# Head output projections behind the next head's value groups, and the retention norm's steps further apart

## The chip, the cores and the metric

The kernel runs on one core of a Trainium2 chip. Its time is the device time of one execution in microseconds (us). Several executions are timed, and the median is quoted; one more execution is recorded by the hardware profiler, and all rows of the trace below come from that one.

## The reference, cut to what matters

Two layers work on 528 tokens (16 learned ones, then 512). Each projects the normed tokens with one large matrix, and has two branches on the slices of that projection: a gated short convolution and a retention with four heads.

```python
proj = rmsnorm(h, pre_norm_g[l]) @ w_in[l] + b_in[l]
c_h, c_b, c_c, c_z, r_q, r_k, r_v, r_z, g_a, g_b = split(proj)
# convolution branch
u = c_c * c_h
y_a = (c_b * (conv_b + taps(u)) * silu(c_z)) @ w_conv_out
# retention branch, for each of 4 heads (256 query/key columns, 512 value columns)
s = (rope(q) @ rope(k).T / 16) * decay       # scores, causal by chunks of 64
out = s @ v                                  # with the carried state
out = (out - mean(out)) * rsqrt(var(out) + 1e-5) * gn_g * silu(z)   # the norm, per token
y_b = concat(out of all heads) @ w_ret_out   # the output projection
# merge
h = h + rmsnorm((sigmoid(g_a) * y_a + sigmoid(g_b) * y_b) @ w_o[l], post_norm_g[l])
```

The mean over the values is taken out of v ahead of the product with the scores, so that the norm only has to find a sum of squares per token and multiply by its inverse root.

## The kernel before

**Precision.** Every product is made in three passes: each operand is split into a rounded high part and the rest (`whi` and `wlo` for weights, a pair `r` for activations). ScalarE casts the high part (L142) and VectorE subtracts it (L143). The three passes are high by high, high by low, and low by high.

**The large projection.** A `Group` makes 256 columns of it (K, Q, the two halves V0 and V1, and the two halves Z0 and Z1 of the gate, for each head; H, C, Z and B for each of four convolution groups). It uses a block scheme with seven products instead of eight. A product is one call of `mul` (L279): 12 matmuls, into the accumulators `pa`, `pb` or `pc`. ScalarE evicts them (`put`, L325, and the copy of bias into `pa`, L335). A Group needs four pairs of split weights, and sums of raw weight blocks that VectorE makes (L307, L314, L315).

**The output projection of a head** is four `RetOut` jobs, RO0 to RO3, of 48 matmuls each in layer 1 (in `mm_tile`, L244, two banks `pp`). It multiplies the normed and split output of the head (`yr`, four pairs `r`) with one pair of split weights.

**The order of the jobs** in a layer is one list, `todo`. For head 1 it reads K, Q, V0, then RO0 and RO1 of head 0, V1, RO2 and RO3 of head 0, Z0, Z1, and likewise for heads 2 and 3. This text calls these ten jobs the group of head 1, 2 or 3. Behind them comes convolution group 1, with the projection of head 3 between its last jobs, then convolution groups 2 and 3. The weights are loaded and split in the order in which the jobs are made: the four Groups of a convolution group first, then the RetOut jobs that stand between them. Six tiles hold raw weights and four pairs hold split ones, so a later load or split waits for a tile to come free.

**Steps of the retention** (rope, scores, product with the values, norm) do not stand in that list. They are queued with `later(n, step)`, and each `mul`, or each two steps of a RetOut product, is a tick; the step is issued n ticks after it was queued. When the last gate half Z1 is done, `z_done` queues the product with the values (`attend`) at ticks 1, 3, 5 and 7, and the norm behind it:

- `stats` at tick 10: a matmul with ones sums the squares over the partitions (L370), VectorE makes the mean (`nv`, L374), GpSimd raises it to the power -1/2 (`ny`, L375);
- `wide` at tick 13: a transpose on TensorE spreads `ny` (L384), ScalarE copies it out (L387);
- `finish(v)` at ticks 14 to 17: VectorE multiplies (L514), and the result is split into a pair `r` (L142, L143), which RO0 to RO3 then read.

A step falls so into the group of the next head: `stats` of head 0 in the group of head 1. The rope of K and Q (L403, L404, L405, then the split into `r`) is queued when K and Q are done; the scores (L422 on TensorE, L433 on VectorE) eight or more ticks behind Q.

**The last word on the order** is a static scheduler's. It takes the program in the order of issue and lays down one list for each engine by its own estimate; evictions by L325, some casts and the end of `attend` have a higher priority there. Each engine then works off its list strictly in that order.

Of the kernel before, what the change touches and what calls it, by code (L numbers as in the profile page):

```python
# [56 lines left out]
def trunk(ctx: ExitStack, tc: tile.TileContext, xT, w_in, binT, w_co, w_ro, w_o, gpre, gpost,  # L57
# [486 lines left out]
    def conv_group(l, i2, res):  # L544
        cs = slice(QCOLS[l].t0, T)
        cc = slice(14 if l else 0, T)
        st = {}

        def c_h(ts):
            st["h"] = ts  # L550

        def c_c(ts):
            st["u"] = []
            for s in range(2):
                u = gr.tile([P, T + 2], F32, tag="u", name=nm("u"), bufs=2)
                if l < DEPTH - 1:
                    nc.vector.memset(u[:, 0:2], 0.0)
                nc.vector.tensor_tensor(u[:, 2 + cc.start:], ts[s][:, cc], st["h"][s][:, cc], op=ALU.mult)
                i = i2 * 2 + s
                a = ts[s]  # L560
                w = lambda j: cw_sb[:, l, j, i:i + 1]
                nc.scalar.activation(a[:, cs], u[:, 2 + cs.start:2 + T], AF.Identity, scale=w(2), bias=cb_sb[:, l, i:i + 1])
                for j in (1, 0):
                    nc.vector.scalar_tensor_tensor(a[:, cs], u[:, j + cs.start:j + T], w(j), a[:, cs], op0=ALU.mult, op1=ALU.add)
                st["u"].append(a)

        def c_z(ts):
            nc.scalar.activation(ts[1][:, cs], ts[1][:, cs], AF.Silu)
            for a, t in zip(st["u"], ts):
                nc.vector.tensor_tensor(a[:, cs], t[:, cs], a[:, cs], op=ALU.mult)  # L570

        def c_b(ts):
            for a, t in zip(st["u"], ts):
                nc.vector.tensor_tensor(t[:, cs], t[:, cs], a[:, cs], op=ALU.mult)
                hi, lo = rslot(), rslot()
                split(hi[:, cs], lo[:, cs], t[:, cs])
                res.append((hi, lo))

        return [Group(l, C_H + i2 * 256, I_CONV[l], c_h), Group(l, C_C + i2 * 256, I_CONV[l], c_c),
                Group(l, C_Z + i2 * 256, I_Q[l], c_z, AF.Silu), Group(l, C_B + i2 * 256, I_Q[l], c_b)]  # L580

    class ConvOut:

# [212 lines left out]
    for l in range(DEPTH):  # L796
# [58 lines left out]
        def z_done(ts, hd, h, l, yr, silu=(1,)):  # L855
# [10 lines left out]
            later(0, start)  # L866
            for v in range(4):
                later(1 + 2 * v, lambda v=v: attend(l, h, *hd["S"], hd["V"], v, hd["zt"][v], hd["sums"]))
            later(10, lambda: hd["n"][0]())
            later(13, lambda: hd["n"][1]())  # L870
            for v in range(4):
                later(14 + v, lambda v=v: hd["n"][2](v))

        hd["done"] = (k_done, q_done, v_done, z_done)
        yrs = jb["yrs"] = [[] for _ in range(H)]
# [7 lines left out]
        for h in range(1, H):  # L883
            d = {}
            add(Group(l, R_K + h * DK, I_ALL[l], lambda ts, d=d: k_done(ts, d)))
            add(Group(l, R_Q + h * DK, I_Q[l], lambda ts, d=d, h=h, l=l: q_done(ts, d, h, l)))
            add(Group(l, R_V + h * DV, I_ALL[l], lambda ts, d=d: v_done(ts, d)))
            for q in (0, 1):
                add(RetOut(l, h - 1, q), yrs[h - 1])
            add(Group(l, R_V + h * DV + 256, I_ALL[l], lambda ts, d=d: v_done(ts, d)))  # L890
            for q in (2, 3):
                add(RetOut(l, h - 1, q), yrs[h - 1])
            for b in range(2):
                add(Group(l, R_Z + h * DV + b * 256, I_Q[l],
                          lambda ts, d=d, h=h, l=l, yr=yrs[h]: z_done(ts, d, h, l, yr), AF.Silu))
        for n, g in enumerate(conv_group(l, 1, conv)):
            add(g)
            if n >= 2:
                for q in (2 * n - 4, 2 * n - 3):
                    add(RetOut(l, H - 1, q), yrs[H - 1])  # L900
        add_conv(2)
        add_conv(3)

        def gate_b(ts, b, l=l):
            cs = slice(QCOLS[l].t0, T)
# [354 lines left out]
```

## Time and profile before

| | us |
|---|---|
| median of three timed executions | 1605.07 |
| lowest and highest of them | 1603.92, 1609.26 |
| the profiled execution | 1600.25 |
| its span in the trace | 1598.4 |

The span runs from the first to the last recorded instruction. In the profiled execution TensorE is busy for 1553.9 us, VectorE for 1168.9 us, ScalarE for 910.2 us and GpSimd for 28.9 us. A busy time is an average over stages that differ; the rows further down are read from single stages. In them a row of the timeline gives a start, a duration, the engine, the line, the operation with the tiles that it writes and reads, and in brackets how long the engine stood idle before it and what ended that.

### The profile page before, as it was taken

How to read it: one execution, taken by the hardware profiler on the slowest of the kernel's cores; microseconds unless marked ns; L12 is line 12 of the kernel's file. 1: busy time of each engine (PE TensorE's matmuls, PEld its weight loads, DVE VectorE, ACT ScalarE, POOL GpSimd, SP SyncE). 2: the span in 40 equal slices, each digit the busy share in tenths (PEclk: the TensorE clock that was granted, in tenths of full speed). 3: DMA queues.
4: the chain of work that ended last, by engine and by line, in shares of the span. 5: the costliest groups of instructions: out<-in, count | busy, mean ns of one | idle time of the engine just before them, and what ended most of it. 6: DMA issues, size and time to landing. Idle time of an engine off the chain costs nothing.

```text
span 1598.4 us, 29227 instructions
## 1 busy us (share of the span) xinstructions
PE 1553.9 (97%) x11762; PEld 1494.1 (93%) x11762; DVE 1168.9 (73%) x1702; ACT 910.2 (57%) x1763; POOL 28.9 (2%) x23
## 2 busy tenths in 40 slices
PE   9999999899999999999999999999999999999998
PEld 9989999898999999999999998998998999999986
DVE  6996966776776788866376889678777777997542
ACT  6675565464565466655345666655654655676531
POOL 0000000001000000000000000000000000000000
PEclk9999999999999999999999999999999999999999
DMA  7132332232222243335321223222322223334421
GB/s 263 67 113 73 106 107 89 83 108 97 89 103 87 91 141 128 133 123 180 119 101 53 100 94 113 103 103 95 111 93 80 101 98 119 132 126 145 142 98 53
DMA packets 86039, 174.37 MB, mean 109 GB/s; under 512 B 11280, under 2 KB 15888, under 8 KB 85904
## 3 DMA queue, kind: packets, MB, share of 16 engines
q1 hardware_dynamic: 85760, 172.50, 31.2%
q8 instruction: 92, 1.51, 0.4%
q14 instruction: 43, 0.35, 0.1%
q10 hardware_dynamic: 144, 0.01, 0.0%
HBM read 168.21 MB, written 4.26 MB: 108 GB/s over the span
## 4 chain that ended last, share of the span: by engine, by line
PE 79%; DVE 10%; ACT 5%; issue 3%; DMA 3%; POOL 1%; SPq 0%; DVEq 0%; POOLq 0%; ACTq 0%
PE pb L279 25%; PE pp L244 15%; PE pc L279 13%; PE pp L648 7%; PE pa L279 6%; PE pp L481 4%; PE pp L1122 3%; PE pb L648 3%; DVE wlo L143 2%; PE pp L422 2%; DMA raw<-in_w_in 2%; ACT whi L142 2%; DVE r L143 1%; PE pp L384 1%; PE pp L447 1%
## 5 line engine op out<-in xcount | busy, mean ns | idle before, releaser
L143 DVE TENSOR_TENSOR wlo<-raw,whi 128x1024 fp32r<-128x1024 f32 (+2 forms) x358 | 392.7, 1107 | 120.4 <-ACT whi L142 117.5
L142 ACT CAST whi<-raw 128x1024 fp32r<-128x1024 f32 (+2 forms) x358 | 339.4, 959 | 227.8 <-PE pp L244 63.7
L279 PE MATMUL pb<-Xh,whi 128*128 128x264 f32 (+2 forms) x1008 | 287.7, 285 | 2.2 <-ACT pa L335 1.2
L279 PE MATMUL pb<-Xl,whi 128*128 128x264 f32 (+2 forms) x1008 | 285.0, 283 | 0.0
L279 PE MATMUL pb<-Xh,wlo 128*128 128x264 f32 (+2 forms) x1008 | 284.7, 283 | 0.1
L244 PE MATMUL pp<-r,whi 128*128 128x264 f32 (+1 forms) x1152 | 251.2, 325 | 5.6 <-ACT r L142 4.8
L279 PE MATMUL pc<-Xh,whi 128*128 128x264 f32 (+2 forms) x672 | 194.4, 289 | 8.1 <-ACT f L325 7.8
L244 PEld LDWEIGHTS pp<-r,whi 128*128 128x128 f32 x1152 | 176.3, 188 | 23.7 <-ACT r L142 5.9
L279 PEld LDWEIGHTS pb<-Xh,whi 128*128 128x128 f32 x1008 | 189.6, 188 | 4.4 <-ACT pa L335 1.6
L279 PE MATMUL pc<-Xl,whi 128*128 128x264 f32 (+2 forms) x672 | 192.0, 286 | 0.0
L279 PE MATMUL pc<-Xh,wlo 128*128 128x264 f32 (+2 forms) x672 | 191.5, 285 | 0.0
L279 PEld LDWEIGHTS pb<-Xl,whi 128*128 128x128 f32 x1008 | 189.6, 188 | 0.6
L279 PEld LDWEIGHTS pb<-Xh,wlo 128*128 128x128 f32 x1008 | 189.3, 188 | 0.5 <-DVE wlo L143 0.3
L244 PE MATMUL pp<-r,wlo 128*128 128x264 f32 (+1 forms) x576 | 153.1, 321 | 1.4 <-DVE wlo L143 1.4
L307 DVE TENSOR_TENSOR raw<-raw 128x512 f32<-128x512 f32 x168 | 115.1, 686 | 41.4 <-DMA raw<-in_w_in 40.9
L279 PEld LDWEIGHTS pc<-Xh,whi 128*128 128x128 f32 x672 | 128.0, 190 | 12.3 <-ACT f L325 11.2
L279 PEld LDWEIGHTS pc<-Xl,whi 128*128 128x128 f32 x672 | 127.9, 190 | 0.4
L279 PEld LDWEIGHTS pc<-Xh,wlo 128*128 128x128 f32 x672 | 127.8, 190 | 0.3
L244 PEld LDWEIGHTS pp<-r,wlo 128*128 128x128 f32 x576 | 95.3, 188 | 9.8 <-DVE wlo L143 2.0
L279 PE MATMUL pb<-Xh,whd 128*128 128x264 f32 (+2 forms) x336 | 96.7, 288 | 1.1 <-ACT f L325 1.1
L279 PE MATMUL pa<-Xh,whi 128*128 128x264 f32 (+2 forms) x336 | 96.7, 288 | 0.0
L279 PE MATMUL pa<-Xl,whi 128*128 128x264 f32 (+2 forms) x336 | 95.7, 285 | 0.0
(219 smaller groups left out, 3300.3 us busy)
## 6 DMA issues: line engine op xcount, KB each, us to landing
raw<-in_w_in SPq DMA_DIRECT2D x426, 256.0 KB, 2.9
raw<-in_w_ro SPq DMA_DIRECT2D x32, 512.0 KB, 3.2
raw<-in_w_in SPq DMA_DIRECT2D x20, 512.0 KB, 4.8
raw<-in_w_co SPq DMA_DIRECT2D x16, 512.0 KB, 3.2
raw<-in_w_o SPq DMA_DIRECT2D x16, 512.0 KB, 3.9
Dsb<-in_decay SPq DMA_DIRECT2D x8, 520.0 KB, 3.9
h1d<-f SPq DMA_DIRECT2D x8, 264.0 KB, 4.5
f<-h1d SPq DMA_DIRECT2D x8, 264.0 KB, 4.3
```

The costliest lines, as they stand in the source:

```text
L142: nc.scalar.copy(dst_hi, src)
L143: nc.vector.tensor_tensor(dst_lo, src, dst_hi.bitcast(F32), op=ALU.subtract)
L244: nc.tensor.matmul(banks[i][:, 0:cols.n], wt(k)[:, msl], xs(k)[:, sl], start=(k == 0 and a == 0), stop=(k == nk - 1 and a == 2),)
L279: nc.tensor.matmul(o[:, 0:n], wt[:, k, :], xs[:, blk, k, HALF - n:], start=(first and k == 0 and a == 0), stop=(k == 3 and a == 2), skip_g ...
L307: nc.vector.tensor_tensor(r[:, 512:], r[:, 512:], r[:, 0:512], op=ALU.add)
L384: nc.tensor.matmul(pp[:, c // per, (c % per) * sc:(c % per + 1) * sc], y[:, c:c + 1].to_broadcast([sc, P]), ident[0:sc, 0:sc], start=True, ...
L422: nc.tensor.matmul(pp[0:kn, n + i, 0:cols.n], k[dt][x][:, k0:k0 + kn] if j < 4 else k8[:, dt * 2 + x, :], q[dt][y][:, sl], start=(dt == 0 ...
L447: nc.tensor.transpose(pp[0:kn, b, v * P:(v + 1) * P], vt[v][:, k0:k0 + kn] if j < 4 else v8[:, v, :], ident)
L481: nc.tensor.matmul(pp[:, b, lo_ - banks[b][0]:hi_ - banks[b][0]], V[j][x][0:kn, v * P:(v + 1) * P], S[0:kn, SOFF[j] + lo_ - q0:SOFF[j] + h ...
L648: nc.tensor.matmul(o, wt(k), xs[:, i0:], start=(k == 0 and a == 0), stop=(k == KD - 1 and a == 2))
L1122: nc.tensor.matmul(o, x[:, xs], wo[k][half][w], start=(k == 0 and a == 0), stop=(k == KD - 1 and a == 2))
```

## The change

Three things are edited. In a head's group, V1 moves ahead of RO0 and RO1, and Z0 stands between RO1 and RO2: the order is now K, Q, V0, V1, RO0, RO1, Z0, RO2, RO3, Z1. In the norm, `stats` goes from tick 10 to 11, `wide` from 13 to 17, and `finish(v)` from 14+v to 18+v. In the convolution part, groups 1 to 3 are one run of twelve Groups, and RO0 to RO3 of head 3 stand one by one behind the fourth to the seventh of them; `conv_group` has become a generator, so that the weights of each Group are queued when its turn comes.

```diff
-        return [Group(l, C_H + i2 * 256, I_CONV[l], c_h), Group(l, C_C + i2 * 256, I_CONV[l], c_c),
-                Group(l, C_Z + i2 * 256, I_Q[l], c_z, AF.Silu), Group(l, C_B + i2 * 256, I_Q[l], c_b)]
+        for col, i0, cb, act in ((C_H, I_CONV, c_h, AF.Identity), (C_C, I_CONV, c_c, AF.Identity),
+                                 (C_Z, I_Q, c_z, AF.Silu), (C_B, I_Q, c_b, AF.Identity)):
+            yield Group(l, col + i2 * 256, i0[l], cb, act)
...
-            later(10, lambda: hd["n"][0]())
-            later(13, lambda: hd["n"][1]())
+            later(11, lambda: hd["n"][0]())
+            later(17, lambda: hd["n"][1]())
             for v in range(4):
-                later(14 + v, lambda v=v: hd["n"][2](v))
+                later(18 + v, lambda v=v: hd["n"][2](v))
...
-            add(Group(l, R_V + h * DV, I_ALL[l], lambda ts, d=d: v_done(ts, d)))
-            for q in (0, 1):
-                add(RetOut(l, h - 1, q), yrs[h - 1])
-            add(Group(l, R_V + h * DV + 256, I_ALL[l], lambda ts, d=d: v_done(ts, d)))
-            for q in (2, 3):
-                add(RetOut(l, h - 1, q), yrs[h - 1])
             for b in range(2):
+                add(Group(l, R_V + h * DV + b * 256, I_ALL[l], lambda ts, d=d: v_done(ts, d)))
+            for b in range(2):
+                for q in (2 * b, 2 * b + 1):
+                    add(RetOut(l, h - 1, q), yrs[h - 1])
                 add(Group(l, R_Z + h * DV + b * 256, I_Q[l],
                           lambda ts, d=d, h=h, l=l, yr=yrs[h]: z_done(ts, d, h, l, yr), AF.Silu))
-        for n, g in enumerate(conv_group(l, 1, conv)):
+        for n, g in enumerate(g for i2 in (1, 2, 3) for g in conv_group(l, i2, conv)):
             add(g)
-            if n >= 2:
-                for q in (2 * n - 4, 2 * n - 3):
-                    add(RetOut(l, H - 1, q), yrs[H - 1])
-        add_conv(2)
-        add_conv(3)
+            if n in (3, 4, 5, 6):
+                add(RetOut(l, H - 1, n - 3), yrs[H - 1])
```

**TensorE, layer 2, group of head 1, between the first and the second product of V0.** `pb` and `pc` are the accumulators of V0, `pp` the two banks of RO0, and `r` the split output of head 0. Before (of 16 rows of L244, the first three and the last two stand here):

```order
L279 MATMUL pb_11706<-Xl,whi_11549 128x264
L279 MATMUL pb_11706<-Xh,wlo_11550 128x264
L244 MATMUL pp_11862<-r_11415,whi_11696 128x512
L244 MATMUL pp_11862<-r_11416,whi_11696 128x512
L244 MATMUL pp_11876<-r_11415,whi_11696 128x512
...
L244 MATMUL pp_11876<-r_11415,wlo_11697 128x512
L244 MATMUL pp_11876<-r_11433,whi_11696 128x512
L279 MATMUL pc_11707<-Xh,whi_11549 128x264
L279 MATMUL pc_11707<-Xl,whi_11549 128x264
```

After, at the same place:

```order
L279 MATMUL pb_11707<-Xl,whi_11545 128x264
L279 MATMUL pb_11707<-Xh,wlo_11546 128x264
L279 MATMUL pc_11708<-Xh,whi_11545 128x264
L279 MATMUL pc_11708<-Xl,whi_11545 128x264
L279 MATMUL pc_11708<-Xh,wlo_11546 128x264
```

The 16 matmuls of RO0 are gone from between the two products, and nothing has taken their place. In layer 1 it is the same with 30 matmuls of L244 (264 columns each). On VectorE, one more sum of weight blocks (L307) stands ahead of the last step of K's rope (L405) there, in both layers.

**TensorE, layer 1, group of head 2, around the sum of squares (L370).** `pc_3263` and `pb_3262` are the last two products of Q before, `pb_3263` the last product of Q after, and `pb_3476` the first product of V0 after. Before:

```order
L279 MATMUL pc_3263<-Xl,whi_3188 128x264
L279 MATMUL pc_3263<-Xh,wlo_3189 128x264
L370 MATMUL pp_3435<-ones_d,f_3148 88x1 x6
L279 MATMUL pb_3262<-Xh,whi_3188 128x264
L279 MATMUL pb_3262<-Xl,whi_3188 128x264
```

After:

```order
L279 MATMUL pb_3263<-Xh,whi_3189 128x264
L279 MATMUL pb_3263<-Xl,whi_3189 128x264
L279 MATMUL pb_3263<-Xh,wlo_3190 128x264
L370 MATMUL pp_3454<-ones_d,f_3149 88x1 x6
L279 MATMUL pb_3476<-Xh,whi_3255 128x264
L279 MATMUL pb_3476<-Xl,whi_3255 128x264
```

The sum of squares stands one product of 12 matmuls later. The spreading transpose (L384) stands directly behind V0's first product in both kernels, so two products lie between the two steps before and one after. The groups of head 3 in layer 1 and of heads 2 and 3 in layer 2 have it so too. In the group of head 1, three products lie between before and six after.

**VectorE, at the same place.** Before:

```order
L405 TENSOR_TENSOR f_3381<-f_3381,f_3382 128x528
L307 TENSOR_TENSOR raw_3326<-raw_3326 128x512
L143 TENSOR_TENSOR wlo_3414<-raw_3040,whi_3413 128x1024
L374 TENSOR_SCALAR nv_3442<-pp_3435 88x6
L143 TENSOR_TENSOR r_3387<-f_3381,r_3386 128x528
L403 TENSOR_TENSOR f_3403<-f_3080,sin_sb 128x528
```

After:

```order
L405 TENSOR_TENSOR f_3381<-f_3381,f_3382 128x528
L143 TENSOR_TENSOR wlo_3414<-raw_3040,whi_3413 128x1024
L143 TENSOR_TENSOR r_3387<-f_3381,r_3386 128x528
L403 TENSOR_TENSOR f_3403<-f_3080,sin_sb 128x528
L374 TENSOR_SCALAR nv_3461<-pp_3454 88x6
L404 TENSOR_TENSOR f_3404<-f_3081,cos_sb 128x528
```

The mean `nv` of the norm now stands behind two steps of the rope of K that it stood ahead of.

## Rows read from the trace of the kernel before

**Rows 1.** The page: busy time of each engine; the chain that ended last.

```profile
PE 1553.9 (97%) x11762; PEld 1494.1 (93%) x11762; DVE 1168.9 (73%) x1702; ACT 910.2 (57%) x1763; POOL 28.9 (2%) x23
PE 79%; DVE 10%; ACT 5%; issue 3%; DMA 3%; POOL 1%; SPq 0%; DVEq 0%; POOLq 0%; ACTq 0%
```

**Rows 2.** Waits of TensorE: who waited for whom, total us, times, longest us.

```profile
PE pc L279 <- ACT f L325: 7.8, 9, 1.6
PE pp L384 <- POOL ny L375: 6.5, 4, 3.0
PE pp L244 <- ACT r L142: 4.8, 4, 1.3
PE pp L370 <- DVE f L496: 4.2, 3, 3.3
```

**Rows 3.** Busy time by stretches, TensorE: us, busy (x matmuls), granted clock, DMA, GB/s.

```profile
600.00:640.00 40.00, 40.00 (x332) 1.00 0.38 131
```

**Rows 4.** The same for PE, PEld, DVE, ACT, POOL, behind three waits of TensorE.

```profile
141.30:148.10 6.80, 6.76 (x35) 6.79 (x36) 4.04 (x6) 2.42 (x5) 1.71 (x1) 0.50 0.11 39
284.70:288.10 3.40, 3.40 (x17) 3.40 (x17) 1.95 (x3) 1.98 (x6) 0.00 (x0) 0.50 0.00 0
1081.00:1085.00 4.00, 4.00 (x36) 4.00 (x35) 3.83 (x6) 3.92 (x11) 0.00 (x0) 1.00 0.00 0
```

**Rows 5.** Timeline, layer 2, group of head 1, around V0's second product (pc).

```profile
973.76 1.08 PE L244 MATMUL pp<-r,whi 128*128 128x512 f32 x4
975.64 0.70 DVE L405 TENSOR_TENSOR f<-f,f 128x528 f32<-128x528 f32 x1
975.77 0.50 PE L244 MATMUL pp<-r,wlo 128*128 128x512 f32 x1 [0.93 <-DVE wlo L143]
976.26 0.68 DVE L307 TENSOR_TENSOR raw<-raw 128x512 f32<-128x512 f32 x1
976.37 0.63 ACT L142 CAST r<-f 128x528 fp32r<-128x528 f32 x1 [2.94 <-DVE f L405]
977.37 0.48 ACT L325 ACTIVATE f<-pc,bin 128x256 f32<-128x256 f32 x1
978.65 0.28 PE L279 MATMUL pc<-Xh,whi 128*128 128x264 f32 x1
```

**Rows 6.** Busy time by stretches, VectorE alone, ahead of that place.

```profile
952.00:976.30 24.30, 24.30 (x35) 1.00 0.38 133
```

**Rows 7.** Timeline, layer 1, group of head 1: sum of squares, then V0's second product.

```profile
141.34 1.89 PE L370 MATMUL pp<-ones_d,f 128*88 128x1 f32 x12 [3.33 <-DVE f L496]
146.98 1.22 DVE L143 TENSOR_TENSOR wlo<-raw,whi 128x1024 fp32r<-128x1024 f32 x1 [2.76 <-ACT whi L142]
176.76 0.48 ACT L325 ACTIVATE f<-pc,bin 128x264 f32<-128x264 f32 x1
177.94 0.28 PE L279 MATMUL pc<-Xh,whi 128*128 128x264 f32 x1
```

**Rows 8.** Timeline, the norm's steps in later groups of both layers.

```profile
275.98 1.07 PE L370 MATMUL pp<-ones_d,f 128*88 128x1 f32 x12 [0.35 <-DVE f L496]
278.34 4.71 POOL L375 TENSOR_TENSOR ny<-nv,mhalf 88x6 f32<-88x6 f32 x1 [132.93 <-DVE nv L374]
283.11 1.57 PE L384 MATMUL pp<-ident,ny 88*128 88x88 f32 x12 [3.01 <-POOL ny L375]
504.63 1.32 POOL L375 TENSOR_TENSOR ny<-nv,mhalf 88x6 f32<-88x6 f32 x1 [108.03 <-DVE nv L374]
1077.54 1.16 PE L384 MATMUL pp<-ident,ny 128*128 128x128 f32 x8 [0.21 <-POOL ny L375]
1080.30 0.39 PE L279 MATMUL pc<-Xh,whi 128*128 128x264 f32 x1 [1.60 <-ACT f L325]
```

**Rows 9.** Timeline, layer 2, group of head 2: RO0 waits for the norm's result.

```profile
1096.32 0.73 PE L244 MATMUL pp<-r,whi 128*128 128x512 f32 x2 [1.28 <-ACT r L142]
```

**Rows 10.** Timeline, layer 1, convolution group 1.

```profile
520.75 0.39 PE L279 MATMUL pb<-Xh,whi 128*128 128x264 f32 x1 [0.61 <-ACT pa L335]
```

## The prediction

> **What bounds the kernel now.** I read the page first, for the engine that is busy longest and for the chain that ended last. TensorE is busy for 1553.9 us of the span of 1598.4 us, and 79% of the chain is TensorE [rows 1]. So the kernel can gain at most the 44.5 us in which TensorE stands idle, plus whatever it does at a reduced clock. Next I read a stretch without a wait: 332 matmuls in 40.00 us, 0.1205 us each, at full clock [rows 3]. That is the price of a product: 12 matmuls, 1.446 us, which is also a tick. The change takes no matmul away and adds none. Its worth is therefore the waits that it removes, less the waits that it makes, plus what the clock does behind them.
>
> The list of TensorE's waits names those that the edits touch [rows 2]: V0's and other Groups' second product (`pc`) waiting for an eviction, 7.8 us in 9 waits; the spread waiting for GpSimd's power, 6.5 us in 4; the output projection waiting for the norm's result, 4.8 us in 4; and the sum of squares waiting for `attend`, 4.2 us in 3, of which one is 3.3 us.
>
> Last I read the clock behind waits [rows 4]. Behind the wait of 3.33 us [rows 7] TensorE ran 6.8 us at 0.50, the lower of its two levels (1.2 GHz of 2.4), and behind the spread's wait of 3.01 us [rows 8] 3.4 us. Half a clock loses half of such a stretch: 3.4 and 1.7 us. Behind the wait of 1.60 us [rows 8] the clock stayed at 1.00 [rows 4]. So a wait of 3 us costs more than itself here, and one of 1.6 us doesn't.
>
> **The change part by part.** Positive is slower, and the sum is made against the profiled execution, 1600.25 us.
>
> *a. Layer 2, group of head 1: the filler goes.* Before, V0's first product is followed by 16 matmuls of RO0, which run from 973.76 to 978.65, 4.89 us, with one wait of 0.93 in them [rows 5]: 3.96 us of work. Only then comes `pc`. In the changed order nothing stands there. Can `pc` start at 973.76 instead? It needs ScalarE to have evicted Q's last use of `pc`. That eviction is at 977.37, in ScalarE's list behind the cast of K's rope at 976.37, and this waits for VectorE's L405 at 975.64 [rows 5]. VectorE was busy for all of the 24.30 us ahead of that [rows 6], so nothing pulls L405 forward. One more L307 stands ahead of it in the new list. VectorE starts such steps 0.62 us apart (975.64 to 976.26) [rows 5], so it costs 0.6. The eviction then ends at 977.37 + 0.48 + 0.6 = 978.45, and `pc` starts at about 978.5. TensorE waits 978.5 − 973.76 = 4.7 us, and the 3.96 us of RO0 must be done later; before, the same stretch took 4.89. Net 4.7 + 3.96 − 4.89 = **+3.8** us. Ends: +3.2 without the extra L307, +4.5 with another such step in the way.
>
> *b. Layer 1, group of head 1: the same, but with something in return.* `stats` at one tick later comes 1.446 us later, so its wait of 3.33 us [rows 7] falls to about 1.9. By the row of 1.60 us that is nearer to the waits without a clock loss, so the 6.8 us at half clock go too. Gain 1.4 + 3.4 = 4.8. Against it the filler is lost here too: 30 matmuls, 30 × 0.1205 = 3.6 us. The eviction ended at 176.76 + 0.48 = 177.24 and `pc` started at 177.94 [rows 7]; with the extra L307 the eviction would end at 177.9 if VectorE kept its times. So `pc` starts no earlier than before unless VectorE comes forward with TensorE. It stood idle for 2.76 us ahead of one weight split [rows 7], the first of two such gaps, waiting for ScalarE and so for tiles that TensorE frees; with TensorE earlier, most of both should go. If `pc` so starts 4 us earlier, at 173.9, that pays for the 3.6 us that are left to do: **0**, with a stall of some 5 us, since V0's first product is then done 4.8 us earlier. Ends: −1, and +3.6 if VectorE does not come forward.
>
> *c. The norm in the groups of heads 2 and 3.* The words of the change promise more room between `stats` and the spread. The new list of TensorE has less: one product between them instead of two, since `stats` moved back by one product and the spread stayed. On VectorE `nv` also falls behind two steps of the rope, 0.7 us each by L405 [rows 5]. So the spread's wait of 3.01 us [rows 8] grows, by the 1.446 of a product, less the 0.35 that `stats` itself had waited [rows 8]: +1.1 in each of the two groups of layer 1. GpSimd's power decides how much of it stays. The same operation took 4.71 us in this place and 1.32 us elsewhere [rows 8], a difference of 3.4; started later, it runs beside other work of VectorE. I take +0.4 for each. In layer 2 the spread waits 0.21 and `pc` behind it 1.60 [rows 8]; a later spread takes from the second wait what it adds to the first: +0.1 each. Sum **+1.0**. Ends: −1 (the power quicker in one of them) and +4 (1.1 in both, and 0.9 in both of layer 2).
>
> What makes the power take 4.71 us in one place and 1.32 us in the other the rows don't say [rows 8]. The Trainium skill, page "GPSIMD Engine Reference", section 1, says that GpSimd shares its interfaces to SBUF with VectorE and that instructions of VectorE with two inputs from SBUF contend with it. By that rule the rope's steps, which have two inputs each, are what the power would be slowed by in its new place too, and c would lie at its upper end.
>
> *d. RO0 no longer waits for the norm; the scores wait for the rope.* In the groups of heads 2 and 3, RO0's four waits of 1.1 to 1.3 us go, 4.8 us in all [rows 2], of which one is shown [rows 9]. But behind V1's first product the new list has the scores of the same head, where RO0's matmuls stood before, and these need Q's rope, another pair that VectorE and ScalarE split last. No row shows this wait. The nearest is the wait that it replaces, on the same two engines, 1.2 us: 4 × 1.2 against 4.8. In the groups of head 1, VectorE and ScalarE gain several us on TensorE while it stalls in a and b just ahead: nothing. **0**. Ends: −4.8 if no score waits, and +4.8 if all six wait for 1.6 us, the longest wait of that kind [rows 2].
>
> *e. Convolution group 1.* The wait of 0.61 us ahead of a Group's product behind RO [rows 10] goes, and a like one of 0.60 in layer 2: **−1.2**. Ends −2 and 0. Queueing the weights one Group at a time moves loads on SP's queue and splits on ScalarE and VectorE, but not ahead of a matmul that waits for them in these rows; the DMA engines are busy for 0.38 of a full stretch [rows 3]. Nothing for that.
>
> *f. The clock behind the new stalls.* The stalls in a and b are 4.7 and some 5 us, longer than the 3.01 that was followed by 3.4 us at half clock. Each should cost 1.7 us. But VectorE is behind TensorE there, and a slower TensorE lets it catch up, so that later waits shrink: I take half of 2 × 1.7, **+1.7**. Ends: 0, and 3.4 + 1.7 = +5.1 if one of them is followed by 6.8 us.
>
> Sum: 3.8 + 0 + 1.0 + 0 − 1.2 + 1.7 = +5.3, that is 1605.6 us for the profiled execution. This stands 4.8 us under the median, so the median should be 1605.07 + 5.3 = **1610.4 us**.
>
> **The rivals.** *R1, faster: VectorE does not bind at V0.* If L405 comes as early as TensorE allows, V0's `pc` waits no longer than such waits do elsewhere, 1.6 us. Then a is 1.6 − 0.93 = +0.7; b is −4.8 + 1.6 = −3.2; d is near its lower end, −4; c and e stay, f is 0: 0.7 − 3.2 + 1.0 − 4 − 1.2 = −6.7, or 1598.4. For it: several waits are removed outright [rows 2]. Against it: VectorE without a gap for 24.30 us [rows 6].
>
> *R2, slower: every new stall drags the clock.* In b VectorE does not come forward (+3.6), and both stalls are followed by half clock to the upper end (+5.1, 3.4 above my term): 5.3 + 3.6 + 3.4 = +12.3, or 1617.4. It decides from a stall of 3 us on, which both are unless VectorE is early; the two stretches at 0.50 [rows 4] speak for it, and that the second stall is only estimated speaks against it. The Trainium skill, page "TensorE: Matmul & The Clock Gate", Part 1, "What's actually happening", says that the throttled state is the default and that activity releases it. By that rule each new stall gives the clock away and the work behind it has to win it back, as the trace has it behind 3.01 us; its result is R2.
>
> *R3, slower: the norm's steps come closer, not further apart.* The change doesn't do there what it says: c at its upper end, +4 instead of +1.0: +8.3, or 1613.4. For it: the order, and 4.71 us of the power [rows 8]. Against it: 1.32 us of the same operation.
>
> **How the numbers follow.** My forecast, 1610.4 with terms near those above, has 0.55; R1 0.22; R2 0.13; R3 0.10. About 0.3% (4.8 us) is what a measurement of this kernel can tell from no change, so the bounds are 1600.25 and 1609.9. The forecast lies half a us beyond the upper one, so its 0.55 is split, 0.30 slower and 0.25 within. R1 gives 0.16 faster and 0.06 within, R2 and R3 are slower but for 0.05. Faster 0.18, within 0.36, slower 0.46. The range takes in most of R1, since −6.7 is 1598.4, and R2, 1617.4: 1598 to 1618. The likeliest case has its own range: a +3.2 to +4.5, b −1 to +3.6, f 0 to +3.4, 1607 to 1616.
>
> **What would show it.** Right: the wait of `pc` for an eviction grows from 7.8 us by 8 to 10 us, with two single waits of about 5 us, near 974 and near 170; the wait of `stats` at 141 falls to about 1.9 with full clock behind it; the spread's waits in layer 1 grow to 3.4 or more; RO's waits for the norm's cast go, and scores wait 1 to 1.5 us for a rope. Wrong: V0's `pc` in the group of head 1 starts right behind `pb` (a, b, f fall, and R1 holds), or the stall is there but the clock stays at 1.00 (f falls), or a wait appears that none of these rows show, above all one for weights that are split too late.

## The result, and the profile after

The changed kernel takes 1617.83 us (median of six executions, 1612.45 to 1619.51), the kernel before 1604.79 beside it. The ratio is 1.007, with a 95% interval of 1.0051 to 1.0088: 0.7% slower, 13.0 us on the medians. The forecast was 1610.4, slower, with a range of 1598 to 1618. Its profiled execution took 1618.11 us; its span is 17.9 us longer than that of before. The spans differ by more than the medians because the profiled execution of before lies 4.5 us under its median and that of the change 0.3 us above.

The page of the changed kernel, the two lines that answer to [rows 1]:

```profile
PE 1560.2 (97%) x11762; PEld 1500.0 (93%) x11762; DVE 1172.0 (73%) x1702; ACT 913.7 (57%) x1763; POOL 23.4 (1%) x23
PE 78%; DVE 12%; ACT 5%; issue 3%; DMA 2%; SPq 0%; DVEq 0%; POOLq 0%; ACTq 0%
```

The work is the same, instruction for instruction in number. TensorE is busy for 6.3 us more although nothing was added: that is work at a reduced clock. It sets these two executions apart rather than the two kernels. The profiled execution of before had a mean granted clock of 0.995; 58 timed executions of the same kernel beside the experiments had 0.9918 on average, and twelve of the change (six here, six in e7) 0.9913. By the missing share of the time, an estimate, the clock costs about 13 us in the one kernel and 14 in the other. Idle time of TensorE is 56.1 us instead of 44.5, and these 11.6 us are close to the 13.0 by which the medians differ: the loss is waiting. In the chain VectorE has grown from 10% to 12%, and GpSimd has gone from it. At full clock a product costs what it did, 332 matmuls in 40.00 us [rows 3]:

```profile
600.00:640.00 40.00, 40.00 (x332) 1.00 0.38 127
```

The waits of TensorE, to be held against [rows 2]:

```profile
PE pc L279 <- ACT f L325: 13.9, 10, 3.4
PE pp L422 <- ACT r L142: 8.5, 6, 1.9
PE pb L279 <- ACT f L325: 7.0, 7, 1.4
PE pb L279 <- ACT pa L335: 2.9, 2, 1.6
PE pp L422 <- DVE r L143: 2.6, 4, 0.7
PE pp L370 <- DVE f L496: 1.9, 1, 1.9
PE pp L384 <- POOL ny L375: 1.6, 4, 0.6
```

What the change was to take away did go: the output projection (L244) no longer waits for the norm's cast (4.8 us), the spread (L384) waits 1.6 us instead of 6.5, the sum of squares (L370) 1.9 instead of 4.2. What came is more: `pc` for evictions +6.1, the scores (L422) 11.1 from nothing, `pb` for evictions 7.0 from 1.1, and for the copy into `pa` 2.9 from 1.2.

**Where the time went.** A ledger by stage says it better than totals. The matmuls of the Groups come in the same order in both kernels, so the first matmul of a Group is a landmark; the table gives how much longer a stage took than before, in us, in one profiled execution of each kernel (e1 to e10 are the experiments below). A stage "head 1" runs from the last Group of convolution group 0 to the first of head 2's group, "heads 2 and 3" from there to convolution group 1; a stage that an edit leaves alone differed by up to 4.0 us between executions (layer 2, heads 2 and 3 in e3, which leaves the heads as they were), so small entries aren't read one by one. The execution of before had the high clock just named, so many entries stand a little too high.

| | layer 1, head 1 | layer 1, heads 2 and 3 | layer 1, conv. 1 | layer 2, head 1 | layer 2, heads 2 and 3 | layer 2, conv. 1 |
|---|---|---|---|---|---|---|
| before, us | 113.5 | 227.7 | 109.9 | 104.7 | 214.5 | 106.1 |
| change | +9.3 | −1.8 | −0.8 | +7.0 | +3.0 | −1.0 |
| change again (e7) | +8.8 | −1.6 | −0.9 | +8.4 | +3.2 | −1.1 |
| e1, jobs only | +8.5 | +4.7 | +0.2 | +7.4 | +10.8 | −0.1 |
| e2, ticks only | −1.5 | +8.9 | −1.1 | +0.3 | +8.9 | −1.0 |
| e3, convolution only | +0.4 | +1.6 | −0.4 | +0.3 | +4.0 | −0.4 |
| e4, head 1 undone | +0.4 | −1.7 | −0.8 | +0.3 | +1.0 | −1.0 |
| e5, K's rope later | +7.2 | −3.0 | −0.8 | +5.4 | +4.4 | −1.1 |
| e6, RO0 back | +2.5 | −1.3 | −1.0 | +2.4 | +4.2 | −1.0 |

16.3 of the 17.9 us stand in the two groups of head 1. In the groups of heads 2 and 3, where the norm and the scores were moved against each other, the balance is +1.2 in all, which is nothing that one execution can tell. They had less to lose at V0: in the kernel before, RO0 did not run between V0's first and second product there. Only the spread stood between them (in layer 2, head 2, at 1077.54, then `pc` at 1080.30 [rows 8]); RO0's first matmul came 8.8 us behind that `pc`, at 1089.10.

**The group of head 1 in layer 2**, the waits of TensorE there (before, the same stretch had the one of 0.93 and the filler, [rows 5]):

```profile
974.15 0.39 PE L279 MATMUL pb<-Xh,whi 128*128 128x256 f32 x1 [1.58 <-ACT pa L335]
987.89 0.40 PE L279 MATMUL pc<-Xh,whi 128*128 128x264 f32 x1 [3.44 <-ACT f L325]
1001.50 1.18 PE L422 MATMUL pp<-r,r 128*80 128x512 f32 x3 [1.88 <-ACT r L142]
1015.02 0.39 PE L279 MATMUL pb<-Xh,whd 128*128 128x264 f32 x1 [1.38 <-ACT f L325]
```

And what the longest of them waits for, on VectorE and ScalarE:

```profile
985.56 0.71 DVE L405 TENSOR_TENSOR f<-f,f 128x528 f32<-128x528 f32 x1
986.36 0.63 ACT L142 CAST r<-f 128x528 fp32r<-128x528 f32 x1 [2.41 <-DVE f L405]
987.36 0.48 ACT L325 ACTIVATE f<-pc,bin 128x256 f32<-128x256 f32 x1
```

Read upwards: `pc` starts at 987.89, when ScalarE's eviction of 987.36 is done. ScalarE had stood idle for 2.41 us ahead of the cast of K's rope, which stands ahead of that eviction in its list, and the cast waited for VectorE's L405. VectorE was busy for 24.86 of the 25 us up to it, from 961 to 986. From L405 to the eviction the chain is that of [rows 5], 1.80 us from start to start against 1.73 before; but before, 16 matmuls of RO0 ran meanwhile, and `pc` started 1.28 us after the eviction did, here 0.53. The waits sum to 8.28 us; less the 0.93 of before that is 7.35, against 7.0 in the ledger.

```profile
961.00:986.00 25.00, 24.86 (x35) 1.00 0.38 128
```

**The group of head 1 in layer 1** (before: [rows 7]):

```profile
142.94 1.22 PE L370 MATMUL pp<-ones_d,f 128*88 128x1 f32 x9 [1.86 <-DVE f L496]
164.46 0.39 PE L279 MATMUL pb<-Xh,whi 128*128 128x264 f32 x1 [1.31 <-ACT pa L335]
178.29 0.59 PE L279 MATMUL pc<-Xh,whi 128*128 128x264 f32 x1 [3.31 <-ACT f L325]
193.87 1.09 PE L422 MATMUL pp<-r,r 128*80 128x264 f32 x4 [1.13 <-ACT r L142]
207.13 0.39 PE L279 MATMUL pb<-Xh,whd 128*128 128x264 f32 x1 [1.12 <-ACT f L325]
215.24 0.96 PE L447 MATMUL pp<-ident,f 128*80 128x128 f32 x7 [1.36 <-ACT YB L538]
```

The clock behind waits, as in [rows 4] (busy times of PE, PEld, DVE, ACT and POOL, then the granted clock): behind the wait of 1.86, behind that of 3.31, behind the spread of head 2's group in layer 1, and behind the wait of 3.44 in layer 2.

```profile
143.20:150.00 6.80, 6.80 (x36) 6.80 (x36) 3.75 (x6) 2.59 (x7) 2.25 (x1) 0.50 0.35 113
177.30:184.10 6.80, 5.81 (x26) 5.81 (x27) 3.62 (x5) 3.94 (x12) 0.00 (x0) 0.50 0.12 39
293.40:296.80 3.40, 3.40 (x18) 3.40 (x17) 0.73 (x2) 2.08 (x7) 0.00 (x0) 0.50 0.02 5
988.00:992.00 4.00, 4.00 (x34) 4.00 (x35) 2.67 (x5) 3.56 (x10) 0.00 (x0) 1.00 0.18 61
```

In layer 1 the new waits are 1.31 + 3.31 + 1.13 + 1.12 + 1.36 = 8.23; the wait of the sum fell by 1.47, and the stretch at half clock behind `pc` costs half of its 5.81 busy us, 2.9. That is 9.7 against 9.3 in the ledger. In e7 the wait of the sum was 2.94 us and both half-clock stretches were 3.4 us long, and the ledger has 8.8.

**The spread** in the group of head 2, layer 1 and then layer 2, to be held against [rows 8]:

```profile
288.98 0.16 DVE L374 TENSOR_SCALAR nv<-pp 88x6 f32<-88x6 f32 x1 [0.42 <-PE pp L370]
289.22 1.72 POOL L375 TENSOR_TENSOR ny<-nv,mhalf 88x6 f32<-88x6 f32 x1 [141.07 <-DVE nv L374]
290.99 1.57 PE L384 MATMUL pp<-ident,ny 88*128 88x88 f32 x12 [0.57 <-POOL ny L375]
293.10 0.39 PE L279 MATMUL pc<-Xh,whi 128*128 128x264 f32 x1 [0.53 <-ACT f L325]
1093.78 1.16 PE L384 MATMUL pp<-ident,ny 128*128 128x128 f32 x8 [0.25 <-POOL ny L375]
1096.16 0.39 PE L279 MATMUL pc<-Xh,whi 128*128 128x264 f32 x1 [1.23 <-ACT f L325]
```

One product less lies between the sum and the spread, as the lists said, and yet the spread waits 0.57 us instead of 3.01: GpSimd's power took 1.72 us instead of 4.71.

### The profile page after: what moved, and what is told of

The parts are those of the page before. It is cut to its first block, busy times and chain, and to the rows that moved or that the text cites. A ratio compares the mean times of both kernels' runs of the same rounds, so it can differ in the third digit from the quotient of the medians.

```text
span 1616.3 us, 29238 instructions
## 1 busy us (share of the span) xinstructions
PE 1560.2 (97%) x11762; PEld 1500.0 (93%) x11762; DVE 1172.0 (73%) x1702; ACT 913.7 (57%) x1763; POOL 23.4 (1%) x23
## 4 chain that ended last, share of the span: by engine, by line
PE 78%; DVE 12%; ACT 5%; issue 3%; DMA 2%; SPq 0%; DVEq 0%; POOLq 0%; ACTq 0%
PE pb L279 24%; PE pp L244 16%; PE pc L279 13%; PE pp L649 6%; PE pa L279 6%; PE pp L481 4%; DVE wlo L143 3%; PE pp L1118 3%; PE pb L649 3%; DMA raw<-in_w_in 2%; ACT whi L142 2%; DVE r L143 1%; ACT f L325 1%; PE pp L447 1%; DVE f L405 1%
## 5 line engine op out<-in xcount | busy, mean ns | idle before, releaser
L143 DVE TENSOR_TENSOR wlo<-raw,whi 128x1024 fp32r<-128x1024 f32 (+2 forms) x358 | 393.9, 1109 | 126.6 <-ACT whi L142 124.7
L244 PE MATMUL pp<-r,whi 128*128 128x264 f32 (+1 forms) x1152 | 249.0, 323 | 0.0
L244 PEld LDWEIGHTS pp<-r,whi 128*128 128x128 f32 x1152 | 177.0, 188 | 15.7 <-ACT YB L538 0.4
L307 DVE TENSOR_TENSOR raw<-raw 128x512 f32<-128x512 f32 x168 | 115.5, 688 | 56.3 <-DMA raw<-in_w_in 55.5
L244 PE MATMUL pp<-r,wlo 128*128 128x264 f32 (+1 forms) x576 | 153.5, 321 | 0.0
L279 PEld LDWEIGHTS pc<-Xh,whi 128*128 128x128 f32 x672 | 128.9, 192 | 18.6 <-ACT f L325 17.9
L244 PEld LDWEIGHTS pp<-r,wlo 128*128 128x128 f32 x576 | 95.6, 188 | 8.1
L279 PE MATMUL pb<-Xl,whd 128*128 128x264 f32 (+2 forms) x336 | 96.3, 286 | 0.0
L279 PE MATMUL pb<-Xh,wld 128*128 128x264 f32 (+2 forms) x336 | 96.2, 286 | 0.0
```

Source lines behind the costliest of these rows:

```text
L143: nc.vector.tensor_tensor(dst_lo, src, dst_hi.bitcast(F32), op=ALU.subtract)
L244: nc.tensor.matmul(banks[i][:, 0:cols.n], wt(k)[:, msl], xs(k)[:, sl], start=(k == 0 and a == 0), stop=(k == nk - 1 and a == 2),)
L279: nc.tensor.matmul(o[:, 0:n], wt[:, k, :], xs[:, blk, k, HALF - n:], start=(first and k == 0 and a == 0), stop=(k == 3 and a == 2), skip_g ...
L307: nc.vector.tensor_tensor(r[:, 512:], r[:, 512:], r[:, 0:512], op=ALU.add)
```

## The experiments

All times are medians beside runs of the kernel before on the same chip, and ratios to it with their 95% intervals.

**e1 and e2: the two halves apart.** e1 has the new order of a head's jobs with the old ticks:

```diff
             add(Group(l, R_V + h * DV, I_ALL[l], lambda ts, d=d: v_done(ts, d)))
-            for q in (0, 1):
-                add(RetOut(l, h - 1, q), yrs[h - 1])
             add(Group(l, R_V + h * DV + 256, I_ALL[l], lambda ts, d=d: v_done(ts, d)))
-            for q in (2, 3):
-                add(RetOut(l, h - 1, q), yrs[h - 1])
             for b in range(2):
+                for q in (2 * b, 2 * b + 1):
+                    add(RetOut(l, h - 1, q), yrs[h - 1])
```

> Only the new order of the jobs in a head's group; the norm's ticks (10, 13, 14+v) and the convolution part are those of before. Theory A (the matmuls of RO0 are missing as filler between V0's first and second product in the group of head 1, while the eviction waits behind K's rope): waits of pc of 3 to 4 us in the groups of head 1 in both layers, time +8 to +13 us against before, about 1613 to 1618. Theory B (the norm's later steps collide with the rope and the evictions on VectorE and ScalarE): with the old ticks no such wait, time within 3 us of before.

Measured: 1633.93 us, ratio 1.0168 (1.0148 to 1.0188), slower by far than the whole change, and beyond the 8 to 13 us of theory A. The ledger has the loss of the groups of head 1 (+8.5 and +7.4, as in the change), and 15.5 us (4.7 and 10.8) more in the groups of heads 2 and 3. The first is theory A. The second neither theory had; the rows of layer 2, head 2, show it:

```profile
1113.10 0.68 DVE L143 TENSOR_TENSOR r<-f,r 128x512 fp32r<-128x512 f32 x1
1113.70 0.68 DVE L403 TENSOR_TENSOR f<-f,sin_sb 128x512 f32<-128x512 f32 x1
1115.51 0.68 DVE L405 TENSOR_TENSOR f<-f,f 128x512 f32<-128x512 f32 x1
1116.95 1.44 PE L422 MATMUL pp<-r,r 128*80 128x512 f32 x2 [4.57 <-ACT r L142]
```

With the old ticks the norm's multiplications and splits (the L143 of 1113.10 is one) stand ahead of the second half of Q's rope on VectorE, and the scores, now directly behind V1's first product, wait 4.57 us for that rope. In the change the same wait is 1.27 us: the later ticks bring the norm's steps behind the rope.

e2 has later ticks with the old order of jobs:

```diff
-            later(10, lambda: hd["n"][0]())
-            later(13, lambda: hd["n"][1]())
+            later(11, lambda: hd["n"][0]())
+            later(16, lambda: hd["n"][1]())
             for v in range(4):
-                later(14 + v, lambda v=v: hd["n"][2](v))
+                later(17 + v, lambda v=v: hd["n"][2](v))
```

> Only the norm's ticks later: 11, 16 and 17+v (one tick less than in the change for the last two, since in the old order of jobs RO0 would else stand ahead of the result that it reads); jobs as before. Theory A: no wait of pc above 2 us in the groups of head 1, the wait of the sum of squares near 141 us falls from 3.3 to 1.9, time -3 to +3 us against before. Theory B: the loss of the groups of head 1 is there, +6 us or more.

Measured: 1619.52 us, ratio 1.0074 (1.006 to 1.0088). The groups of head 1 lose nothing (−1.5 and +0.3), so theory B falls for them. But heads 2 and 3 lose 17.8 us: RO0 stands where it stood, the norm's result comes later, and RO waits for it, twice as long as before.

```profile
PE pp L244 <- ACT r L142: 9.7, 4, 2.5
PE pp L384 <- POOL ny L375: 8.3, 4, 3.8
```

The waits themselves are the smaller part: TensorE is idle for 6.0 us more in these two stages. The clock costs the rest, some 14 us: eight stretches at half clock stand there, where the profile of before has two. Two of them, behind a spread's wait and behind one of RO:

```profile
402.50:409.30 6.80, 6.80 (x31) 0.50 0.13 49
1105.70:1109.10 3.40, 3.02 (x10) 0.50 0.45 128
```

That is no accident of one execution. The mean granted clock over e2's five is 0.985, against 0.992 for the kernel before beside them, which is worth about 11 of e2's 11.6 us by the same estimate; for e1 it is 0.988, about 7 of its 26.

So each half alone costs 12 to 26 us, nearly all or much of it in heads 2 and 3, and together they cancel there. The loss of the groups of head 1 belongs to the order of the jobs alone.

**e3: the convolution part alone**, with jobs and ticks of the heads as before:

```diff
-        for n, g in enumerate(conv_group(l, 1, conv)):
+        for n, g in enumerate(g for i2 in (1, 2, 3) for g in conv_group(l, i2, conv)):
             add(g)
-            if n >= 2:
-                for q in (2 * n - 4, 2 * n - 3):
-                    add(RetOut(l, H - 1, q), yrs[H - 1])
+            if n in (3, 4, 5, 6):
+                add(RetOut(l, H - 1, n - 3), yrs[H - 1])
```

> Only the convolution part: RO0 to RO3 of head 3 behind the fourth to seventh convolution Group, weights queued one Group at a time. Both theories: -1 to -2 us (two waits of 0.6 us go), within what can be told from no change. If the later queueing of weights matters, +2 us or more with waits for weight splits.

Measured: 1607.74 us, ratio 1.0007 (0.9993 to 1.002): no change that can be told. Its stages of convolution group 1 are 0.4 us shorter in each layer.

**e4: the whole change except in the group of head 1.** The old order of jobs for `h == 1`, the old ticks for head 0's norm:

```diff
-            later(11, lambda: hd["n"][0]())
-            later(17, lambda: hd["n"][1]())
+            later(11 if h else 10, lambda: hd["n"][0]())
+            later(17 if h else 13, lambda: hd["n"][1]())
...
+            if h == 1:
+                add(Group(l, R_V + h * DV, I_ALL[l], lambda ts, d=d: v_done(ts, d)))
+                for q in (0, 1):
+                    add(RetOut(l, h - 1, q), yrs[h - 1])
...
```

> The whole change, except that in the group of head 1 of each layer the old order of jobs and, for head 0's norm, the old ticks are kept. Theory C (all of the loss arises in the two groups of head 1; in those of heads 2 and 3 what is won at the spread is lost again at the scores): -2 to +2 us against before, 12 to 14 us faster than the change. Rival D (the loss is spread over all groups by a TensorE that runs closer to VectorE): +4 us or more against before.

Measured: 1601.39 us, ratio 0.997 (0.9957 to 0.9983): 6.5 us faster than before by the medians, and 1.0% faster than the change by the ratios. Theory C holds: all of the loss arises in the two groups of head 1. It came out a little better than C said, since the rest of the change is a gain.

**e5: is it ScalarE's list?** In the group of head 1 the second half of K's rope is queued three ticks later. TensorE's list there is that of the change; on ScalarE the cast now stands behind the evictions.

```diff
-        def k_done(ts, hd):
+        def k_done(ts, hd, e=2):
...
-            later(2, b)
-            later(3, k8)
+            later(e, b)
+            later(e + 1, k8)
...
+            add(Group(l, R_K + h * DK, I_ALL[l], lambda ts, d=d, e=5 if h == 1 else 2: k_done(ts, d, e)))
```

> The whole change, but in the group of head 1 the second half of K's rope is queued three ticks later. TensorE's list in that group is the same as in the change; in ScalarE's list the cast of that half now stands behind the evictions of Q's accumulators instead of ahead of them. Theory E (V0's second product waits because the eviction stands behind the rope's cast on ScalarE, which waits for VectorE): the two waits of pc of 3.3 to 3.4 us fall below 1.7, time 3 to 7 us below the change (ratio to before about 1.003 to 1.005). Rival F (VectorE's load alone sets the pace there): the wait only moves to the next eviction or to the scores, the two groups together stay within 2 us of the change (ratio 1.006 to 1.008).

Measured: 1612.87 us, ratio 1.0035 (1.0019 to 1.0051), 5.3 us below the change, which was run beside it as e7 (1618.15, ratio 1.0065, 1.0047 to 1.0083).

```profile
PE pp L422 <- ACT r L142: 10.3, 6, 2.3
PE pc L279 <- ACT f L325: 7.5, 9, 1.2
PE pb L279 <- ACT pa L335: 4.1, 2, 2.7
```

The two waits of 3.3 and 3.4 us are gone, none of `pc` is longer than 1.2: theory E is right on their cause. But the scores wait 1.8 us more for ScalarE than in the first profile of the change, and the waits for the copy into `pa` are 1.2 us more, the longest 2.7. In the ledger the two groups keep 12.6 of 16.3 us. So rival F has its part: with the knot on ScalarE undone, VectorE's load moves some of the wait to the next place.

**e6: only the filler back.** RO0 alone stands between V0 and V1 again in the group of head 1; the rest of the change stays, its ticks too.

```diff
                 add(Group(l, R_V + h * DV + b * 256, I_ALL[l], lambda ts, d=d: v_done(ts, d)))
+                if h == 1 and not b:
+                    add(RetOut(l, 0, 0), yrs[0])
             for b in range(2):
-                for q in (2 * b, 2 * b + 1):
+                for q in (2 * b, 2 * b + 1)[h == 1 and not b:]:
```

> The whole change, but in the group of head 1 RO0 alone stands between V0 and V1 again; the norm's new ticks stay. 16 matmuls of RO0 come back between V0's first and second product in layer 2. Theory A (missing filler): the wait of pc there falls from 3.4 to below 1 us, the group's excess over before falls by at least 4 us in each layer, time -8 to -13 us against the change, ratio to before 0.999 to 1.002. If the new ticks of head 0's norm matter too, RO0 waits for the norm's cast by 1 us or more and half of the loss stays, ratio 1.003 to 1.005.

Measured: 1604.59 us, ratio 0.998 (0.9969 to 0.9991), 13.6 us below the change. One job moved in each of two groups undoes the loss. In layer 2 the one wait in front of `pc` is RO0's for its weights, as in [rows 5]; what the two groups keep, 2.5 and 2.4 us, is for the most part waits for split weights further on, the longest in layer 1:

```profile
976.02 0.50 PE L244 MATMUL pp<-r,wlo 128*128 128x512 f32 x1 [1.32 <-DVE wlo L143]
222.06 0.39 PE L279 MATMUL pb<-Xh,wlo 128*128 128x264 f32 x1 [1.70 <-DVE wlo L143]
```

Not all of the 13.6 us is the filler. TensorE's idle time is 48.5 us, 7.6 less than in the first profile of the change and 10.4 less than in e7's, and 4.0 more than before. The mean granted clock over e6's twelve executions is 0.995, against 0.991 for the change, an estimated 6 to 7 us. So by these figures e6 beats the kernel before by its clock and not by its waits; why its clock is higher was not tried.

**e7: the change again.**

> The change itself once more, beside the others on the same chip: ratio to before 1.005 to 1.009. Whether half-clock stretches stand at the same places as in the first profile: if they follow the waits alone, the same six; if not, the ones behind waits under 2 us differ.

Measured: 1618.15 us, as said. Six of its stretches at half clock stand near those of the first profile (at 145, 179, 292, 405 and 825 us, and at the end), the first two of them half as long; three do not (855, 988 and 1111 us), and the one near 1218 us of the first profile is missing. One of these is behind the same wait of layer 2 that left the clock at 1.00 in the first profile. The wait in the timeline of e7, and the busy times and the clock behind it:

```profile
988.15 0.40 PE L279 MATMUL pc<-Xh,whi 128*128 128x264 f32 x1 [3.45 <-ACT f L325]
```

```profile
988.40:991.80 3.40, 3.40 (x17) 3.40 (x17) 1.16 (x2) 2.03 (x7) 0.00 (x0) 0.50 0.19 66
```

**e9: the sum's tick alone.** The kernel before with `later(11, ...)` for the sum of squares instead of 10.

> The kernel before with one number changed: the sum of squares at tick 11 instead of 10; the spread (13), the rest of the norm and all jobs as before. On TensorE and VectorE the sum, the mean and the spread stand as in the change. Theory G (the later sum lets GpSimd's power be short, 1.4 to 1.7 us instead of 2.6 to 4.7, because VectorE pauses ahead of the mean): the spread's four waits fall from 6.5 us to under 2 in all, time -3 to -7 us against before. Rival H (the power was short in the change only because the jobs around it moved): powers of 2.6 us and more stay, the spread's waits grow by up to 1.4 us each, time 0 to +4 us.

Measured: 1608.04 us, ratio 1.0005 (0.9996 to 1.0013). Each theory has half of it. Layer 1, head 2 (the mean, then the power), and layer 2, head 2:

```profile
278.20 0.16 DVE L374 TENSOR_SCALAR nv<-pp 88x6 f32<-88x6 f32 x1
278.44 3.47 POOL L375 TENSOR_TENSOR ny<-nv,mhalf 88x6 f32<-88x6 f32 x1 [131.11 <-DVE nv L374]
1079.59 0.16 DVE L374 TENSOR_SCALAR nv<-pp 128x4 f32<-128x4 f32 x1 [0.57 <-PE pp L370]
1079.83 1.41 POOL L375 TENSOR_TENSOR ny<-nv,mhalf 128x4 f32<-128x4 f32 x1 [125.54 <-DVE nv L374]
```

Where VectorE ran without a pause up to the mean, the power took 3.47 us; where it stood idle for 0.57 us ahead of it, 1.41. In the change it stood idle for 0.42 us there. So the gain at the spread was not the later tick as such; by these rows it went with VectorE being at the mean before TensorE was done with the sum.

**e8 and e10: faster versions.** e8 is e4 with the scores of heads 2 and 3 queued two ticks later (10 instead of 8), e10 is e8 with the sum at tick 11 for head 0 too.

```diff
-            add(Group(l, R_Q + h * DK, I_Q[l], lambda ts, d=d, h=h, l=l: q_done(ts, d, h, l)))
+            add(Group(l, R_Q + h * DK, I_Q[l], lambda ts, d=d, h=h, l=l: q_done(ts, d, h, l, 10 if h > 1 else 8)))
...
-            later(11 if h else 10, lambda: hd["n"][0]())
+            later(11, lambda: hd["n"][0]())
```

> The version with the group of head 1 undone, and in the groups of heads 2 and 3 the scores queued at ticks 10, 12, 14 instead of 8, 10, 12. The first scores stay where they were on TensorE, the later ones move behind one more product of V1. If the waits of V1's later products for evictions (four of about 1.1 us) come from the scores' place: -2 to -4 us against that version, ratio to before 0.994 to 0.996. If not: within 1.5 us of it, ratio about 0.997.

> The fastest version so far (group of head 1 undone, scores of heads 2 and 3 two ticks later) with the sum of squares of head 0 at tick 11 too. Its wait near 141 us should fall from 3.7 to about 2 us: -1.5 us against that version, and -3.4 more if the half-clock stretch of 6.8 us behind it goes. The change itself has that wait at 1.9 with the half clock still behind it, which speaks for -1.5 alone: ratio to before about 0.994 to 0.996.

Measured: e8 1601.03 us, ratio 0.9952 (0.9934 to 0.9969); e10 1599.3 us, ratio 0.9944 (0.9928 to 0.9959). e10 beats both kernels: it is 8.6 us below the kernel before that ran beside it, and 1.2% below the change by the ratios. In e8 the waits of V1's products for evictions fell as expected, from 4.6 to 1.1 us, but others came, and idle time was 43.4 us against 44.0. In e10 the wait of the sum near 141 us is 1.6 instead of 3.7, as expected, and the stretch at half clock near it is 3.4 us long instead of 6.8. The rows stand in the order e4, e8 (two), e10:

```profile
PE pb L279 <- ACT f L325: 4.6, 5, 1.1
PE pb L279 <- ACT f L325: 1.1, 2, 0.8
PE pp L370 <- DVE f L496: 3.7, 1, 3.7
PE pp L370 <- DVE f L496: 1.6, 1, 1.6
```

The steps from e4 to e8 and from e8 to e10 are smaller than their intervals; that each of them gains is not shown.

## Why the prediction was right, and where its sizes were not

The sign and the place were right: slower, because V0's second product in the group of head 1 waits behind K's rope when RO0 is no longer there to fill the time (a, b). e6 and e4 show the first, e5 the way through ScalarE. The sum was +5.3 and the medians gave +13.0. That is 0.2 us inside the range and outside the 1607 to 1616 of the likeliest case; the range reached so far for the sake of R2, whose price is not what the runs show, so that it held is partly luck. The chances carry a slip: the parts named add up to 0.16 faster and 0.48 slower, where 0.18 and 0.46 stand. Term by term, in the order of the prediction, with the measured sizes from the ledger:

- **a, +3.8 forecast, +7.0 measured.** The wait of `pc` was 3.44 us, not 4.7, but a wait of 1.58 us for the copy into `pa` had come ahead of it, and the two together, 5.02 us, are near the forecast. The step that failed is to take the stall for the only new wait: 1.88 us (scores) and 1.38 (`pb` of V1) came behind it in the same group. The working looked at one pair of products and took the rest of the group as unchanged, though RO0 and RO1 had moved out of V0 and V1 altogether.
- **b, 0 forecast, +9.3 measured** (with the layer 1 part of f). The loss was foreseen, the return was not there. Counted from the start of its stage, `pc` started 1.2 us earlier than before, not 4: VectorE hardly came forward. The wait of the sum fell from 3.33 to 1.86 us as said, but the stretch at half clock did not go: 6.8 us at 0.50 stand behind it, as before. The step that failed is taking 1.86 us for a wait that leaves the clock alone because one of 1.60 had. The profiles of the other kernels say more: with the sum at tick 10 (before, e1, e3, e4, e8) the stretch was 6.8 us each time; at tick 11 it was 6.8 in the change and e2, 3.4 in e6, e7, e9 and e10, and absent in e5, behind a wait of 2.45 us (rows below the list). So on average a little under half of the 3.4 us came back.
- **c, +1.0 forecast; the spread's waits fell by 4.9 us.** The order was read rightly, one product less in between, and the conclusion was wrong in sign: the power took 1.72 us instead of 4.71. The lower end had allowed for one shorter power. The Trainium skill's rule on the page "GPSIMD Engine Reference", section 1, speaks of contention with VectorE's two-input instructions; such steps ran beside the power in both kernels, at 4.71 and at 1.72 us, so by that alone the two would not differ.
- **d, 0 forecast.** RO's 4.8 us of waits went, and 11.1 us at the scores came, 3.0 of them in the groups of head 1, where I had put nothing since VectorE would have caught up. It had not. The upper end, +4.8, was too low. Waits of V1's `pb` for evictions, about 1.1 us in each of these four groups, were in no row and no term. c and d together: +1.2 us in the four groups of heads 2 and 3, against +1.0; the errors cancel there, and the agreement is luck.
- **e, −1.2 forecast, −1.8 measured** in the two stages of the change; e3 alone shows no difference that can be told.
- **f, +1.7 forecast.** Behind the wait of layer 1 the clock was at 0.50 for 6.8 us, 2.9 us lost, and for 3.4 us in e7; behind that of layer 2 it was lost in e7 and not in the first profile. So the price is about right for the two stalls. But over whole executions the change lost hardly more to the clock than the kernel before (0.9913 and 0.9918): counting only the clock behind new stalls, against one execution of before at 0.995, was the step that failed.

The sum of squares in e5, and TensorE and its clock from there on (b):

```profile
142.57 1.07 PE L370 MATMUL pp<-ones_d,f 128*88 128x1 f32 x12 [2.45 <-DVE f L496]
142.50:149.00 6.50, 6.43 (x57) 1.00 0.33 93
```

R1 fell with the rows of VectorE, again all but without a gap. R3's premise held (the two steps are closer), its price did not. R2 named the time, 1617.4, and half of its reasons: VectorE hardly came forward in b. Its price for the clock, 3.4 us over f, is not in the mean clocks. The rule of the Trainium skill on the page "TensorE: Matmul & The Clock Gate", Part 1, "What's actually happening", that the default is the throttled state and activity releases it, agrees with the loss in layer 1; the wait of 3.44 us without a loss, and of 3.45 with one, shows that the length of the wait does not settle it.

What stays open: why the clock fell at 293.4 behind waits of 0.57 and 0.53 us, why e6 runs at a higher clock than the other versions and e2 at a lower one, and how the 5.3 us that e5 leaves against before divide between VectorE's load and the clock.

## What to carry to other kernels

Work that stands between two steps of a chain is cover: before moving it, follow what the step behind it waits for, through every list on the way, and ask what stands in the gap afterwards; here one small job, put back in two places, was worth 13.6 us, half or more of it in waits. A move in the order of jobs and a move in the delays of the steps that feed them are to be tried together, since each alone may cost (15.5 and 17.8 us in heads 2 and 3 here) what both together do not. One profiled execution can stand at another clock than most: hold its granted clock against the mean of the timed ones before reading its busy time as the kernel's. And the same pattern may suit some repetitions and not the first: heads 2 and 3 were no worse for the change, head 1, where the job had been the filler, was.

## What the runs showed of the hardware that I had not expected

GpSimd's power on six columns took 1.32 to 4.71 us by its record. In the groups of heads 2 and 3, its end stood 1.18 us behind the end of some instruction on VectorE (0.88 us on the four columns of layer 2). With VectorE idle ahead of the mean, it was the first instruction beside the power (1.72 us in the change, 1.41 in layer 2); with VectorE running through into the mean, it was the last one ahead of VectorE's next pause (4.71 before, 3.47 in e9). Spans on GpSimd are rough, but the spread on TensorE started 0.05 us behind that end in the change as in [rows 8], so the wait was real. Why the pause ahead matters was not tried.

The clock was the other surprise. Two executions of one kernel had the same wait at the same place, 3.44 and 3.45 us, and kept the full clock in the one and lost half of it for 3.4 us in the other. And two versions that differ little in their waits, e2 and the kernel before (47.9 and 44.5 us of idle time), differ in their mean granted clock, 0.985 and 0.992 over their timed executions.
